# Three units of three experts in a new sequence, large GpSimd operations on VectorE, first unit mapped in order of use

## The chip, the core and the metric

The kernel runs on one core of one Trainium2 chip. The metric is device time in microseconds of one execution, from the median of several runs; less is better. The engines are named as in the profile: PE (TensorE), DVE (VectorE), ACT (ScalarE), POOL (GpSimd), SP (SyncE, which here issues most transfers).

## The reference

One layer of a diffusion backbone for 128 context tokens and 256 latent tokens (T = 384, D = 1024), in float32. A modulated input goes through a projection, four mLSTM heads and four Fourier groups, an output projection, and a LayerNorm; the second half is a routed mixture of 32 experts, four for each token, and a second LayerNorm.

```python
mix = jnp.concatenate([h_m, f_m], axis=-1) @ w_out
x = layer_norm(DEEPNORM_ALPHA * x + gate1 * mix, ln1_w, ln1_b)
u2 = x * (1.0 + scale2) + shift2
...
logits = xt.astype(F32) @ router_w.astype(F32) + router_b.astype(F32)
top_val, top_idx = lax.top_k(logits, TOP_K)
gates = jax.nn.softmax(top_val, axis=-1)
...
h = xblk @ w_gu[e] + b_gu[e]
x_glu, x_lin = jnp.split(h, 2, axis=-1)
x_glu = jnp.minimum(x_glu, SWIGLU_LIMIT)
x_lin = jnp.clip(x_lin, -SWIGLU_LIMIT, SWIGLU_LIMIT)
act = x_glu * jax.nn.sigmoid(SWIGLU_ALPHA * x_glu) * (x_lin + 1.0)
return act @ w_down[e] + b_down[e]
...
x = layer_norm(DEEPNORM_ALPHA * x + gate2 * y, ln2_w, ln2_b)
```

The modulation (shift, scale, gate) comes from SiLU(cond) through a linear map, with one cond for context tokens and one for latent tokens. Each expert has w_gu of 1024 x 2048 (8 MB) and w_down of 1024 x 1024 (4 MB).

## The kernel before

**Front, 0 to 244 us.** The projections run with the operands split into a high part and a low part (fp32r), three products for each. `halves_of` splits the input projection's weights (ACT L119, DVE L120); `wo_split(i, part)` does it for w_out: eight high halves as copies on ACT (L247), eight low halves as subtractions of 128x1024 on POOL (L249). `proj_N(3, ...)` computes the output gate's projection and calls three groups of work between its matmuls: Fourier stages (`fourier_A`, `fourier_B`), the heads' norms, `mod_rest` and `wo_split`. `mod_rest` (L668 to L674) makes the second half's modulation rows in a small tile `sm` on DVE and writes them to memory (`dab`) from ACT's queue, to be read back as rows broadcast over all partitions. `heads_T` transposes the gated heads (PE L597). The output projection (L853) is worked off as rows of eight steps for three token blocks (0 is the context) and two column halves; `out_half` adds the residual (DVE L860, L862, L864), `out_norm` normalises (ACT), and for block 0 the map with context scale and shift follows in two halves on POOL (L886, L887). `turn` transposes for the router, `router` multiplies (L918), `top4` picks four experts (DVE L923 to L946), `places` counts (PE L950, L951), `places_0` and `gather_0` (L977, L985) gather the tokens of experts 0 and 1, the first unit, so that they can start before the sort is done. The order of the steps from there on is written out as a string of step names (L1016).

**Places and units.** The experts 2 to 31 are sorted by their number of tokens and fill 30 places of fixed capacity; experts 0 and 1 have the first two. Capacities are grouped to units of 128 slots:

```python
KINDS = dict(A=[128], B=[96, 32], C=[64, 64], D=[64, 32, 32], E=[32] * 4)
SEQUENCE = "DACBACBACBACACCE"
```

The first unit, [64, 64], stands ahead of the sequence: 17 units, 32 places. A place ranks by its capacity, so the sequence sets when an expert of which size runs. Its weights are fetched through registers loaded with its number.

**Expert loop, L1327 to L1410.** For place i: SP queues the gate/up weights of place i + 2 (`load_gu`, four pieces of 2 MB) and the down weights of place i + 1 (`load_dn`, two pieces of 2 MB), all of them issued at L755 into a ring of eight slots of 2 MB; an issue waits until PE has finished with the piece that was in its slot. PE computes `gate_up` of place i (L1163, its bias L1171 or L1167), `spread` of finished units back to the tokens (L1241, added by DVE L1246; for the first unit with the experts' down bias, L1239), and `down` of place i - 1 (L1222). A unit's tokens are gathered two units at a time (`gather_two`, L1107). The first unit's gathered tokens are mapped with scale and shift (`modulate`, ACT L796 for the first four blocks of 128 rows, DVE L794 for the other four, and an addition of the context part, L797); expert 0 multiplies them in the order 2, 3, 0, 1, 4 to 7.

For expert 0 the second half of the down weights lies outside the ring, in two tiles of other pools (`w0` and `y1`, L781 and L782); the first half takes ring slots.

**Final rows.** At place 28 (i == NE - 4) a ring slot is taken for `fb`, four rows broadcast over the partitions for the last norm. A transfer of one element per partition into it (L1353) marks it as written, and at the end of the place `final_row` fills it (PE L1309 into PSUM, ACT L1310 into fb):

```python
if i == NE - 4:
    fb = slot(4, 1024, hold=True)[0]
    SP.dma_start(fb[:, 0, 0:1], bcast(ln2_w[:, 0:1]))
```

`fold` (L1317 to L1321, on DVE and POOL) folds the residual into the sum, `last_down` and `spread_last` (L1414, L1394) end the last place.

## Time and profile before

| | |
|---|---|
| median of 3 runs | 1246.8 us (1244.35, 1246.8, 1248.54) |
| profiled execution, own time | 1248.78 us |
| its span | 1247.1 us |
| PE busy | 1167.6 us (94%) |
| DVE, ACT, POOL busy | 446.4, 229.0, 69.3 us |
| read from HBM | 448.91 MB |
| mean transfer rate over the span | 363 GB/s |
| expert 0's first matmul | 244.17 us |

The times in the rows below are microseconds from the start of the span. A row of a timeline has the start, the duration, engine, line of the kernel, operation, what is written and read by the program's names, and in brackets how long the engine stood idle before and on whom it waited. The share of busy time is a mean over stages with different limits: the stages are told apart by the answers by stretches, which give each engine's busy time, the granted clock of PE (1.00 is 2.4 GHz, 0.50 is 1.2 GHz) and what the transfers moved. The waits of SP's queue tell why a transfer is not issued earlier.

### The profile page before, as it was taken

Reading aid. Unit: us, or ns where it says so; the run is one execution under the profiler, and the core shown is the slowest. Engines: PE = TensorE matmul, PEld = TensorE weight load, DVE = VectorE, ACT = ScalarE, POOL = GpSimd, SP = SyncE. Lnnn points to the kernel's source line nnn. Section 1 sums busy time; section 2 is a strip of 40 time slices with the busy share of each in tenths; the row PEclk is TensorE's granted clock in tenths of the full one; section 3 lists DMA queues with packets and bytes.
Section 4 is the critical chain, followed back from the end, with each engine's and each line's share of the span. In section 5 each row is a group of like instructions: output and inputs, shape, how many; then the busy total and the mean of one; then the engine's idle time right before and its main releaser. Section 6 shows DMA issues by size and latency. Waiting matters only on the chain.

```text
span 1247.1 us, 16409 instructions
## 1 busy us (share of the span) xinstructions
PE 1167.6 (94%) x6628; PEld 556.8 (45%) x6628; DVE 446.4 (36%) x944; ACT 229.0 (18%) x418; POOL 69.3 (6%) x79
## 2 busy tenths in 40 slices
PE   7999989799999999999999999999999999993874
PEld 4876768535335433434343353334435345331321
DVE  4444684623112431414323142332234124130415
ACT  2333341311211110201111121011111111111112
POOL 2001042200000000000000000000000000000301
PEclk9999989899899999999999999999999999996988
DMA  9977546499999999999999999999999899999993
GB/s 324 391 277 263 216 174 255 156 389 406 404 416 417 416 417 417 416 407 414 415 362 409 414 363 358 419 416 362 363 417 398 301 391 403 406 418 403 401 410 118
DMA packets 96978, 452.71 MB, mean 363 GB/s; under 512 B 8308, under 2 KB 18760, under 8 KB 62084
## 3 DMA queue, kind: packets, MB, share of 16 engines
q1 hardware_dynamic: 95088, 450.04, 91.0%
q10 hardware_dynamic: 1268, 1.31, 0.3%
q8 instruction: 54, 0.88, 0.3%
q0 software_dynamic: 544, 0.29, 0.1%
q14 instruction: 24, 0.20, 0.0%
HBM read 448.91 MB, written 2.70 MB: 362 GB/s over the span
## 4 chain that ended last, share of the span: by engine, by line
PE 84%; DMA 7%; DVE 5%; ACT 2%; issue 1%; SPq 1%; ACTq 0%; DVEq 0%
PE b L1163 38%; PE b L1222 19%; PE b L1241 4%; PE p L422 3%; DMA w<-in_w_gate_up_dram 3%; PE b L1107 3%; PE b L1171 2%; PE pm L853 2%; DMA w<-in_ln_w_dram 2%; PE b L1196 2%; DMA w<-in_w_ada_dram 1%; PE k L353 1%; ACT y L1228 1%; PE a L220 1%; DVE y L1230 1%
## 5 line engine op out<-in xcount | busy, mean ns | idle before, releaser
L1163 PE MATMUL b<-w,XT 128*64 128x512 f32 (+1 forms) x2560 | 496.2, 604 | 30.5 <-ACT w L1310 19.7
L1163 PEld LDWEIGHTS b<-w,XT 128*64 128x64 f32 (+1 forms) x2560 | 143.6, 129 | 332.2 <-issue 294.4
L1222 PE MATMUL b<-w,aT 128*64 128x512 f32 (+1 forms) x1596 | 248.3, 515 | 3.3 <-DMA w<-in_w_down_dram 3.2
L1182 DVE TENSOR_SCALAR g<-b 128x512 f32<-128x512 f32 (+1 forms) x40 | 24.5, 612 | 373.7 <-PE b L1171 293.9
L1222 PEld LDWEIGHTS b<-w,aT 128*64 128x64 f32 (+1 forms) x1596 | 81.6, 128 | 156.7 <-issue 141.9
L1230 DVE SCALAR_TENSOR_TENSOR y<-b,gc,y 64x512 fp32r<-64x512 f32 (+1 forms) x88 | 57.4, 652 | 217.6 <-ACT y L1228 217.3
L1228 ACT ACTIVATE y<-b,gc 64x512 fp32r<-64x512 f32 (+2 forms) x100 | 58.7, 587 | 292.1 <-PE b L1222 254.6
L1183 ACT ACTIVATE b<-g 128x512 f32<-128x512 f32 (+1 forms) x40 | 21.5, 538 | 353.6 <-DVE g L1182 353.4
L1246 DVE TENSOR_TENSOR yacc<-yacc,b 128x512 f32<-128x512 f32 x90 | 55.0, 680 | 0.0
L1107 PE MATMUL b<-O,tH 128*128 128x256 f32 x192 | 47.7, 289 | 4.5 <-DVE y L1230 4.5
L1241 PE MATMUL b<-y,OT 128*128 128x512 f32 x192 | 49.9, 405 | 0.0
L1317 POOL TENSOR_TENSOR XT<-tL,tH 128x384 f32<-128x384 f32 x2 | 2.0, 1006 | 841.5 <-PE b L1163 841.5
L1107 PE MATMUL b<-O,tL 128*128 128x256 f32 x192 | 46.5, 283 | 0.0
L1241 PEld LDWEIGHTS b<-y,OT 128*128 128x128 f32 x192 | 35.7, 193 | 13.9 <-issue 5.9
L1107 PEld LDWEIGHTS b<-O,tH 128*128 128x128 f32 x192 | 36.7, 191 | 10.2 <-DVE y L1230 5.3
L120 DVE TENSOR_TENSOR lw<-w,hw 128x1024 fp32r<-128x1024 f32 x20 | 24.4, 1222 | 34.9 <-ACT hw L119 34.7
L1107 PEld LDWEIGHTS b<-O,tL 128*128 128x128 f32 x192 | 36.7, 191 | 0.0
L1171 PEld LDWEIGHTS b<-bgu,pick 128*128 128x128 f32 x224 | 28.0, 189 | 18.7 <-issue 18.7
L1197 ACT ACTIVATE aT<-b 128x512 f32<-128x512 f32 (+1 forms) x40 | 21.3, 534 | 76.2 <-PE b L1196 70.9
L853 PE MATMUL pm<-w,mH 128*128 128x512 f32 x96 | 33.0, 426 | 0.0
L1171 PE MATMUL b<-bgu,pick 128*128 128x256 f32 x224 | 32.8, 292 | 0.0
L422 PE MATMUL p<-hw,uH 128*128 128x512 f32 x72 | 29.7, 412 | 1.7 <-ACT kq L412 1.7
(380 smaller groups left out, 1086.5 us busy)
## 6 DMA issues: line engine op xcount, KB each, us to landing
w<-in_w_gate_up_dram SPq DMA_DIRECT2D x113, 2048.0 KB, 13.4
w<-in_w_down_dram SPq DMA_DIRECT2D x52, 2048.0 KB, 15.5
w<-in_w_gate_up_dram SPq DMA_DIRECT2D x30, 1024.0 KB, 13.5
w<-in_w_down_dram SPq DMA_DIRECT2D x22, 1024.0 KB, 16.6
w<-in_w_ada_dram SPq DMA_DIRECT2D x8, 2048.0 KB, 7.6
w<-in_w_ada_dram SPq DMA_DIRECT2D x8, 1024.0 KB, 8.9
w<-in_w_in_dram SPq DMA_DIRECT2D x4, 2048.0 KB
w<-in_w_out_dram SPq DMA_DIRECT2D x2, 2048.0 KB, 8.8
```

The costliest lines, as they stand in the source:

```text
L422: PE.matmul(p[b], x, y, start=(k == 0 and t == 0), stop=(k == 7 and t == 2))
L853: PE.matmul(pm, x, y, start=(n == 0 and t == (part == 0) and part != 1), stop=(n == 7 and t == 2 and part != 0))
L1107: PE.matmul((pl if b else pc)[:, jj], t[b][:, (2 * i + jj) * 128:(2 * i + jj + 1) * 128], O[:, b], start=(b < 2 and q == 0), stop=(b != 1 ...
L1163: PE.matmul(p[g_][m * h:m * h + m], XT[:, k, o:o + m], rhs, start=(n_ == 0), stop=False, skip_group_check=True)
L1171: PE.matmul(p[g_][:, 256 * h:256 * h + 256], pick[2][:, h], bgu[:, q, 256 * g_:256 * g_ + 256], start=False, stop=(q == 1), skip_group_che ...
L1182: DVE.tensor_scalar(g, pg_, LIMIT, None, op0=OP.min)
L1196: PE.transpose(p[:, cc], s["act"][i][:, cc * 128:(cc + 1) * 128], ident)
L1222: PE.matmul(q[m * h:m * h + m, :f], aT[:, k, o:o + m], w[:, h * f:(h + 1) * f], start=(k == 0), stop=(k == 7))
L1228: ACT.activation(hi if plain else hi.bitcast(FR), dst, AF.Copy, scale=g)
L1230: DVE.scalar_tensor_tensor(y[1][o:o + m, h * f:(h + 1) * f].bitcast(FR), dst, g, hi, op0=OP.mult, op1=OP.subtract)
L1241: PE.matmul(p, OT[:, b * 128:(b + 1) * 128], y[q][:, hf * 512:(hf + 1) * 512].bitcast(FR), start=(u != 0 and q == 0), stop=(q == 1))
L1246: DVE.tensor_add(a, a, p)
```

## The change

The sequence of units is written anew: the unit of four experts (E) is gone, and there are three units of three (D), second, ninth and last; the multiset of capacities (five of 128, three of 96, fifteen of 64, nine of 32) is as before. The low halves of w_out are subtracted on DVE instead of POOL, six of them somewhat later; `mod_rest` stands ahead of two Fourier stages; the context map is two steps X and Y on DVE; O1 and g10 stand ahead of P2; expert 0's down weights are queued in the other order; the first unit is mapped ahead of the bias table's split, blocks 2 and 3 first; the one-element transfer into fb is a memset on POOL.

```diff
@@ -35,8 +35,8 @@
 
 
 
-KINDS = dict(A=[128], B=[96, 32], C=[64, 64], D=[64, 32, 32], E=[32] * 4)
-SEQUENCE = "DACBACBACBACACCE"
+KINDS = dict(A=[128], B=[96, 32], C=[64, 64], D=[64, 32, 32])
+SEQUENCE = "DACBACADBACCACBD"
 PARTS = {32: [(0, 4)], 64: [(0, 2)], 96: [(0, 2), (64, 4)], 128: [(0, 2), (64, 2)]}
 
 
@@ -246,7 +246,7 @@
         if part == 0:
             ACT.activation(h, w, AF.Copy)
         else:
-            POOL.tensor_sub(l, w, h.bitcast(FT))
+            DVE.tensor_sub(l, w, h.bitcast(FT))
 
     todo = [f for name in "qvzo" for f in halves_of(win[name])]
     cut = []
@@ -692,10 +692,9 @@
         head_out(2)
         for i in range(2):
             wo_split(i, 0)
-            wo_split(i, 1)
-        proj_N(3, ev_o, lambda: (mod_loads(), fourier_B(0), fourier_A(2), head_norm(1), head_out(3), wo_split(2, 0), wo_split(2, 1), wo_split(3, 0), wo_split(3, 1)),
-               lambda: (fourier_B(1), fourier_A(3), mod_rest()),
-               lambda: (fourier_B(2), head_norm(2), head_norm(3), fourier_B(3)))
+        proj_N(3, ev_o, lambda: (mod_loads(), fourier_B(0), fourier_A(2), head_norm(1), head_out(3), wo_split(2, 0), wo_split(3, 0)),
+               lambda: (mod_rest(), fourier_B(1), fourier_A(3), wo_split(2, 1), wo_split(3, 1)),
+               lambda: (fourier_B(2), head_norm(2), head_norm(3), fourier_B(3), wo_split(0, 1)))
         ACT.dma_start(new_n[0, 0].rearrange("d h p -> h d p"), nn.rearrange("h (d p) -> h d p", d=2))
         bc = {}
 
@@ -709,6 +708,7 @@
         for gr in range(4):
             split(fo[gr], mH[:, 4 + gr], mL[:, 4 + gr])
         heads_T()
+        wo_split(1, 1)
         wo[1].append(ring(8, 512).bitcast(FR))
         for i in range(4, 8):
             wo_split(i, 0)
@@ -773,7 +773,7 @@
                 src = w_dn[0, ex, :, i * 512:(i + 1) * 512].rearrange("o (k p) n -> p (o k) n", p=128)
                 WT["d", j, i] = fill(slot(8, 512), src, parts)
             return
-        for i in range(2):
+        for i in (1, 0) if j == ORDER[0] else (0, 1):
             src = w_dn[0, ex, i * 512:(i + 1) * 512].rearrange("o (k p) n -> p (o k) n", p=128)
             if i and j == ORDER[0]:
 
@@ -882,9 +882,14 @@
             nc_ = p2.tile([128, D], FT, name="g1c")
             ACT.activation(nc_, tX[b], AF.Identity, bias=nm, scale=rs_)
             ACT.dma_start(dx, nc_)
-            for hs in halves:
-                POOL.tensor_mul(tX[b][:, hs], nc_[:, hs], bc["A", 1][:, hs])
-                POOL.tensor_add(tX[b][:, hs], tX[b][:, hs], bc["D", 1][:, hs])
+            context.append(nc_)
+
+        context = []
+
+        def context_map(hf):
+            hs = halves[hf]
+            DVE.tensor_mul(tX[0][:, hs], context[0][:, hs], bc["A", 1][:, hs])
+            DVE.tensor_add(tX[0][:, hs], tX[0][:, hs], bc["D", 1][:, hs])
 
 
         def fold_1():
@@ -1011,9 +1016,9 @@
 
         m2_, h2, t1, t2 = out_rows(2, 1, {}, 1), out_half(2, 1), top4(1), top4(2)
         steps = dict(m=lambda: (next(m2_, 0), next(m2_, 0)), h=lambda: next(h2, 0), a=lambda: next(t1, 0), b=lambda: next(t2, 0),
-                     A=lambda: weave(t1), B=lambda: weave(t2), S=sort_1, C=lambda: DVE.tensor_copy(cnts, pp[:32, 3]), E=experts)
+                     A=lambda: weave(t1), B=lambda: weave(t2), S=sort_1, X=lambda: context_map(0), Y=lambda: context_map(1), C=lambda: DVE.tensor_copy(cnts, pp[:32, 3]), E=experts)
         next(m2_)
-        for step in "P0 m m T1 m O0 R1 m g00 N1 h h T2 g01 a h a h a N2 a a a a R2 P1 b b b b b b b O1 P2 g11 A g10 O2 B C S g20 g21 E".split():
+        for step in "P0 m m T1 m O0 X R1 m g00 Y N1 h h T2 g01 a h a h a N2 a a a a R2 P1 b b b O1 b b b b g10 P2 A g11 O2 B C S g20 g21 E".split():
             if step in steps:
                 steps[step]()
             else:
@@ -1030,6 +1035,16 @@
         itm = late2.tile([32, 2, ITEMS], FT, name="itm")
         iti = late2.tile([1, ITEMS + 1], I32, name="iti")
         mo = ctx.enter_context(tc.tile_pool(name="mo", bufs=2, reuse_waits="tile"))
+        XT0 = mo.tile([128, 2, 8, 128], FT, name="XT", bufs=1)[:, 0]
+
+        for i, j in ((0, 2), (0, 3), (1, 4), (1, 5), (2, 2), (0, 0), (0, 1), (1, 6), (1, 7), (2, 0), (2, 4), (2, 6)):
+            p, a = xt[j // 4][:, j % 4], [aff[:, q, j:j + 1] for q in range(2)]
+            if i == 0:
+                ACT.activation(XT0[:, j], p, AF.Identity, bias=a[0], scale=a[1])
+            elif i == 1:
+                DVE.tensor_scalar(XT0[:, j], p, a[1], a[0], op0=OP.mult, op1=OP.add)
+            else:
+                DVE.tensor_add(XT0[:, j:j + 2], XT0[:, j:j + 2], xc[j // 4][:, j % 4:j % 4 + 2])
 
         bgu = mo.tile([128, 2, 512], FR, name="bgu", bufs=1)
         raw = mo.tile([128, 512], FT, name="aT", bufs=1)
@@ -1043,9 +1058,6 @@
         POOL.dma_start(rows[0:4], dab[3].rearrange("c (h n) -> (c h) n", h=2))
         POOL.dma_start(rows[4:6], ln2_w.rearrange("o (h n) -> (o h) n", h=2))
         POOL.dma_start(rows[6:8], ln2_b.rearrange("o (h n) -> (o h) n", h=2))
-        XT0 = mo.tile([128, 2, 8, 128], FT, name="XT", bufs=1)[:, 0]
-        for i in range(2):
-            modulate(XT0[:, 4 * i:4 * i + 4], 4 * i, xt[i], xc[i], i)
         sort_1b()
 
 
@@ -1350,7 +1362,7 @@
         if i and i + 2 < NE:
             if i == NE - 4:
                 fb = slot(4, 1024, hold=True)[0]
-                SP.dma_start(fb[:, 0, 0:1], bcast(ln2_w[:, 0:1]))
+                POOL.memset(fb[:, 0, 0:1], 0.0)
             list(load_gu(ORDER[i + 2]))
         if i and i + 1 < NE:
             load_dn(ORDER[i + 1])
```

On DVE, around `mod_rest` in the projection of the output gate, before (`sm` are the modulation rows, `W` the folded Fourier tables, `og` the gated heads, `p_...` the gate's projection in PSUM):

```order
L671 COPY sm<-sm 64x32
L672 COPY sm<-sm 32x32
L673 TENSOR_TENSOR sm<-sm 32x32
L625 TENSOR_TENSOR W_1362<-a,y_1356 128x129
L626 TENSOR_TENSOR W_1362<-a,y_1356 128x127
L625 TENSOR_TENSOR W_1362<-a,y_1356 128x65
L626 TENSOR_TENSOR W_1362<-a,y_1356 128x63
L591 TENSOR_SCALAR og<-nm,mv 128x128 x6
L625 TENSOR_TENSOR W_1383<-n,y_1377 128x129
L626 TENSOR_TENSOR W_1383<-n,y_1377 128x127
L625 TENSOR_TENSOR W_1383<-n,y_1377 128x65
L626 TENSOR_TENSOR W_1383<-n,y_1377 128x63
```

The same stretch after, from the third operation on `sm` on, with the low halves of w_out (`w<-w`, L249) in it:

```order
L671 COPY sm<-sm 64x32
L672 COPY sm<-sm 32x32
L673 TENSOR_TENSOR sm<-sm 32x32
L625 TENSOR_TENSOR W_1323<-a,y_1317 128x129
L626 TENSOR_TENSOR W_1323<-a,y_1317 128x127
L625 TENSOR_TENSOR W_1323<-a,y_1317 128x65
L626 TENSOR_TENSOR W_1323<-a,y_1317 128x63
L249 TENSOR_TENSOR w<-w 128x1024 x2
L625 TENSOR_TENSOR W_1360<-a,y_1354 128x129
L626 TENSOR_TENSOR W_1360<-a,y_1354 128x127
L625 TENSOR_TENSOR W_1360<-a,y_1354 128x65
L626 TENSOR_TENSOR W_1360<-a,y_1354 128x63
```

The operations on `sm` stand ahead of the Fourier pieces L625 and L626 that they stood behind, and two subtractions follow the first of these; a third stands ahead of L492, five more behind L600.

On ACT, the queue that holds the transfer of the modulation rows (`dab<-sm`), before, with two of the Fourier copies (L621) and the table load of the gate's activation:

```order
L621 ACTIVATE y_1314<-a 128x194
L612 ACTIVATE E<-n 128x388
L674 DMA dab<-sm 64x5x32
L621 ACTIVATE y_1356<-a 128x194
L128 ACTIVATE mv<-mv,cst 128x3
L129 ACTIVATE mv<-mv 128x3
L128 ACTIVATE mv<-mv,cst 128x3
L129 ACTIVATE mv<-mv 128x3
L621 ACTIVATE y_1377<-n 128x194
L491 ACT_TABLE_LOAD
```

And after:

```order
L674 DMA dab<-sm 64x5x32
L621 ACTIVATE y_1317<-a 128x194
L612 ACTIVATE E<-n 128x388
L621 ACTIVATE y_1354<-a 128x194
L128 ACTIVATE mv<-mv,cst 128x3
L129 ACTIVATE mv<-mv 128x3
L128 ACTIVATE mv<-mv,cst 128x3
L129 ACTIVATE mv<-mv 128x3
L621 ACTIVATE y_1375<-n 128x194
L491 ACT_TABLE_LOAD
```

The transfer stands ahead of one more L621 and of L612, where it stood behind them; the rest is in the order of before.

On DVE, behind the sort of block 0 (`O_1490<-cst,code` are the places of a block's tokens in the first unit, `tX_69` is the context block), before:

```order
L867 BN_AGGR m_1475<-s_1476 128x2
L976 SCALAR_TENSOR_TENSOR code<-pp,sel 128x32
L977 TENSOR_TENSOR O_1490<-cst,code 128x128
L860 TENSOR_TENSOR pm<-pm,g_1502 128x512
L862 SCALAR_TENSOR_TENSOR tX_71<-tX_71,pm 128x512
L923 SCALAR_TENSOR_TENSOR tiny<-csb,m_1475,lg 128x32
```

And after:

```order
L867 BN_AGGR m_1475<-s_1476 128x2
L981 SCALAR_TENSOR_TENSOR code<-pp,sel 128x32
L982 TENSOR_TENSOR O_1490<-cst,code 128x128
L891 TENSOR_TENSOR tX_69<-g1c,prep 128x512
L892 TENSOR_TENSOR tX_69<-tX_69,Dc 128x512
L891 TENSOR_TENSOR tX_69<-g1c,prep 128x512
L892 TENSOR_TENSOR tX_69<-tX_69,Dc 128x512
L860 TENSOR_TENSOR pm<-pm,g_1502 128x512
L862 SCALAR_TENSOR_TENSOR tX_71<-tX_71,pm 128x512
```

The four operations of the context map, which stood on POOL (L886 and L887), stand here between the places of block 0 and L860 of block 2.

## Rows read from the trace of the kernel before

**Rows 1.** The page, part 1: busy time of each engine.

```profile
PE 1167.6 (94%) x6628; PEld 556.8 (45%) x6628; DVE 446.4 (36%) x944; ACT 229.0 (18%) x418; POOL 69.3 (6%) x79
```

**Rows 2.** Answer by stretches: window, length, busy per engine, PEclk, DMA share, GB/s.

```profile
275.00:625.00 350.00, 347.77 (x1961) 140.82 (x1958) 102.80 (x209) 49.59 (x90) 0.00 (x0) 0.98 1.01 413
330.00:348.00 18.00, 18.00 (x32) 5.42 (x32) 0.00 (x0) 2.99 (x5) 0.00 (x0) 0.53 1.01 418
625.00:1075.00 450.00, 447.77 (x2532) 186.35 (x2530) 140.68 (x279) 62.71 (x112) 0.00 (x0) 1.00 0.96 384
1150.00:1175.00 25.00, 24.03 (x212) 9.09 (x204) 5.85 (x12) 5.87 (x14) 11.27 (x12) 0.94 0.95 379
1175.00:1211.00 36.00, 25.45 (x152) 8.30 (x152) 14.14 (x22) 4.70 (x10) 1.63 (x2) 0.91 1.02 416
1222.00:1247.00 25.00, 8.03 (x32) 2.79 (x28) 15.59 (x27) 4.39 (x10) 5.88 (x4) 0.76 0.17 66
```

**Rows 3.** Waits of SP's queue, 625 to 1075 us: total, times, longest.

```profile
SPq L755 <- PE b L1163: 244.2, 61, 15.4
SPq L755 <- PE b L1222: 132.8, 31, 9.7
```

**Rows 4.** Timeline of PE: first matmuls of places 10 and 20, both 128.

```profile
531.03 3.65 PE L1163 MATMUL b<-w,XT 128*64 128x512 f32 x16
...
855.00 3.65 PE L1163 MATMUL b<-w,XT 128*64 128x512 f32 x16
```

**Rows 5.** Waits of ACT, 1100 to 1200 us.

```profile
ACT w L1310 <- DMA w<-in_ln_w_dram: 22.4, 1, 22.4
```

**Rows 6.** Timeline of PE: first matmul of place 29.

```profile
1149.35 4.66 PE L1163 MATMUL b<-w,XT 128*32 128x512 f32 x24 [19.71 <-ACT w L1310]
```

**Rows 7.** Timeline of all engines, 160 to 179 us.

```profile
161.91 1.19 DVE L120 TENSOR_TENSOR lw<-w,hw 128x1024 fp32r<-128x1024 f32 x1
...
163.18 9.51 POOL L249 TENSOR_TENSOR w<-w 128x1024 fp32r<-128x1024 f32 x4 [36.41 <-DVE lw L120]
...
170.30 2.43 DVE L671 COPY sm<-sm 64x32 f32<-64x32 f32 x1
...
172.76 0.17 DVE L672 COPY sm<-sm 32x32 f32<-32x32 f32 x1
...
173.95 0.33 ACT L621 ACTIVATE y<-a 128x194 f32<-128x194 f32 x1 [10.93 <-DVE sm L673]
...
176.81 1.56 ACT L491 ACTIVATE p<-p 128x512 f32<-128x512 f32 x3
...
178.17 0.48 PE L597 MATMUL n<-cst,og 128*128 128x128 f32 x1 [5.75 <-DVE og L492]
```

**Rows 8.** Chain of waits, 140 to 262 us: start, duration, step.

```profile
205.88 2.10 PE pm L853 x9
...
222.34 3.05 PE pm L853 x8
```

**Rows 9.** Timeline of all engines, 214 to 246 us.

```profile
217.11 1.03 DVE L932 SCALAR_TENSOR_TENSOR sel<-tiny,cst 128x32 f32<-128x32 f32 x1
...
221.24 0.56 PE L950 MATMUL pp<-sel,cst 128*128 128x32 f32 x2 [2.89 <-DVE sel L940]
...
228.64 0.70 DVE L860 TENSOR_TENSOR pm<-pm,g 128x512 f32<-128x512 f32 x1 [3.99 <-PE pm L853]
...
233.58 0.24 DVE L932 SCALAR_TENSOR_TENSOR sel<-tiny,cst 128x32 f32<-128x32 f32 x1
...
234.92 0.58 PE L950 MATMUL pp<-sel,cst 128*128 128x32 f32 x2 [1.72 <-DVE code L976]
...
244.17 2.67 PE L1163 MATMUL b<-w,XT 128*64 128x512 f32 x8 [3.14 <-issue]
```

**Rows 10.** Timeline of PE: down matmuls (L1222) of places 1 and 2, 64 slots each.

```profile
311.38 7.09 PE L1222 MATMUL b<-w,aT 128*64 128x512 f32 x32
...
342.51 9.62 PE L1222 MATMUL b<-w,aT 128*64 128x512 f32 x32
```

## The prediction

> **What bounds the kernel now.** I read the page's busy table first [rows 1]: PE is busy 94% of the span, which would call it the bound everywhere; but that is an average, and the stages have to be taken apart. The answer by stretches does that [rows 2]. From 275 us to 625 us the transfers run at 413 GB/s, from 625 to 1075 at 384, at 1175 to 1211 at 416. PE is busy through all of it (447.77 of 450 us in the second stretch). At 416 GB/s an expert's six pieces of 2 MB (four of gate/up, two of down: 12.58 million bytes) take 30.2 us. The weights are all in at about 1222 us; the 25 us behind that move 66 GB/s and are the tail. So the end is set by when the last weight lands, and that moves only by what the transfers lose: 450 x (1 - 384/416) = 34.6 us in the middle, 25 x (1 - 379/416) = 2.2 us at 1150 to 1175, 2.5 us from 275 to 625, and with whatever shifts the start of the expert loop at 244 us.
>
> Why do transfers pause while the queue has more to fetch? The waits of SP's queue say it [rows 3]: in 625 to 1075 its weight issues wait 61 times for a gate/up matmul (L1163) and 31 times for a down matmul (L1222), that is for a ring slot that PE has not released. In that stretch PE is behind the stream. Elsewhere it is ahead.
>
> So the order of the units matters: PE spends about the same on each unit of 128 slots, the stream spends 30.2 us on each expert, and a unit holds one to four experts. Two starts of a unit A [rows 4] lie six units apart (A C B A C B): (855.00 - 531.03) / 6 = 54.0 us of PE for a unit. A (one expert) puts PE 54.0 - 30.2 = 23.8 us further behind the stream, B and C (two) 6.4 us further ahead, D (three) 36.6 us ahead, E (four) 66.8 us ahead. What the stream loses is the highest point that this balance reaches.
>
> **The change part by part. Sequence.** Balance after u units holding n experts: 54.0u - 30.2n, the first unit (two experts) included. Before, D A C B A C B A C B A C A: the highest point is after 14 units and 24 experts, 756.0 - 724.8 = 31.2 us. That this is the right account is seen in the 34.6 us that the middle stretch loses [rows 2]. After, D A C B A C A D B A C C A: the highest point is after eight units and 14 experts, 432.0 - 422.8 = 9.2 us; D and B bring it to -34, and the last A ends, after 14 units and 25 experts, at 756.0 - 755.0 = 1.0. Gain: 31.2 - 9.2 = **22.0 us**. The measured loss exceeds the balance by 3 to 6 us (34.6, or 37.1 with the first stretch, against 31.2); if the new peak has the same excess the gain stays 22, if the excess vanishes it is 28. Downwards: behind the new peak the balance falls by 43 us, and the ring's eight slots of 2 MB hold 40 us of stream, so PE will wait for weights some 3 us in the new D and B; it stands at 4 instead of 1 after the last A, still under 9.2, and costs nothing. I take 22, bounds 11 (the new peak is twice as high, PE's unit costing 55.4 us in those eight) and 28.
>
> **The placeholder of the final rows.** At place 28 PE stands still for 19.71 us behind ACT L1310, which waits 22.4 us for a one-element transfer of ln2_w (L1353) that is queued behind weights [rows 5, 6]. A memset on the idle POOL takes its place; it waits for nothing but the old user of that slot, which was consumed long before. The standstill goes, but PE is ahead of the stream there, so only the slots it released late count: the 2.2 us of [rows 2] at 1150 to 1175. I take **2.2**, bounds 0 (PE then waits for the same weights) and 5.
>
> **The front, first part (163 to 184 us).** While POOL does four low halves of w_out (9.51 us, 2.4 us each), a copy of 64x32 on DVE takes 2.43 us, and 0.17 us once POOL is done [rows 7]. The small operations of mod_rest take 9 us in this way; ACT's queue holds a transfer from mod_rest's result ahead of its L621, which waits 10.93 us, and behind that come the table load and the gate's activation; PE idles 5.75 us before L597. The change takes the low halves from POOL and puts the transfer ahead of two L621 in ACT's queue. What is late next is the end of the projection itself at 172.4: from ACT's L491 to PE's L597 it is 178.17 - 176.81 = 1.36 us, so PE resumes near 173.9, 4.3 us earlier. What is added to DVE: eight subtractions of 1.19 us [rows 7]. Two lie before the gate in DVE's idle time behind the shortened mod_rest, one between W and L492, and five (6 us) ahead of the first L860; the rows that wait for that one, the turns at 196 us, are 7 us away, so they cost nothing while that margin lasts, up to 1.4 if it doesn't. Behind such gaps PE runs at the lower clock (1.2 GHz) for a while: in the one at 221 us eight L853 take 3.05 us, where nine took 2.10 [rows 8], so 1.2 us are lost each time. With a gap of 1.5 us that may go or stay. I take **5.5**, bounds 0 and 7 (the whole gap and the clock).
>
> **The front, second part (214 to 244 us).** The context map on POOL lies beside top4 of block 0: L932 takes 1.03 us there and 0.24 without POOL, with L934 and L936 some 2.9 us in all; PE's L950 waits 2.89 us for it [rows 9]. As steps X and Y on DVE the map comes behind the sort of block 0, where DVE waited 3.99 us for PE (four operations of 128x512 like the 0.70 us of L860, 2.8 us: they fit): gain 2.9. The half clock behind that gap gives 1.2 [rows 8]. The gather g10 (1.05 us) fills 1.72 us in which PE waits for block 2's positions, less 0.4 for O1 now in the middle of that chain: 0.6. Expert 0 starts 3.14 us after PE's last sort step, because ACT splits the bias table first and then maps k = 0 to 3 in one go, while expert 0 begins with k = 2, 3; now those are mapped first, two operations and one addition of a pair after the last gather: I estimate 1.8 of the 3.14 [rows 9]. Together **6.5**, bounds 3 and 8. What this moves back is the bias split; its first reader is the bias matmul at 262 us, 20 us on. Down weights of expert 0: the halves that need no ring slot go out first; the other four megabytes wait for PE's slots anyway, nothing either way. Of the front PE's time is the path (slots of the ring are released by PE's L853 and L1163), so its 12.0 us pass to the end one for one.
>
> Sum: 22.0 + 2.2 + 5.5 + 6.5 = 36.2 us off the profiled run's 1248.78 gives 1212.6. That run lay 2.0 over the median of 1246.8; against the median the forecast is **1211**.
>
> The Trainium skill has a rule that speaks against this. "SBUF — State Buffer", section "A bandwidth-pool intuition that's wrong", gives HBM to one core about 358 GB/s; by it an expert takes 35.1 us, no unit order would leave PE behind, and the sequence would give nothing (1233). The stretches at 413 to 418 GB/s [rows 2] decide against it.
>
> **Rivals.** (a) *The front gives little* (3 us): something else ends the two gaps, say the transfers of the modulation rows or the added DVE work. For it: three engines hand over within 2 us there. 1211 + 9 = 1220. (b) *The sequence gives half*: the new peak is near 20 us, since four of the eight units ahead of it are the first ones, with the sort and the first spread beside them, and the 54.0 us of a later unit don't show these. 1222. (c) *Half clock in the new D units.* In the first D, PE ran at 0.53 of full clock from 330 to 348 us, the down of 32 matmuls in 9.62 us instead of 7.09 [rows 2, 10]: about 9 us in 18. In the middle D that makes 1 + 3 + 9 = 13 after the last A, 4 above the peak; in the last D it lies before the tail, up to 9. 1215 to 1224, say 1219. Against it: the stretch in the first D follows the spread of the first unit with its 32-row bias matmuls (L1239), which the other D units lack; the E at the end, waiting for weights, had 0.94 and 0.91 [rows 2]. The Trainium skill ("TensorE: Matmul & The Clock Gate", section "HAM oscillation — how this bites in real kernels") says that short bursts of matmuls between waits for transfers start each at the low clock; by it this case is the one. The 0.94 at 1150 to 1175 [rows 2] disagrees. (d) *Slower.* PE at half clock through the whole middle D and B: 108 us there become longer by a factor between 1.36 (9.62/7.09) and, if all of it slows by the clock, 1/0.53 = 1.89, by 39 to 96 us. After the last A the balance is then 43 to 100, and the stream loses 34 to 91 us more: 1245 to 1302, about 1265 in between. It decides for slower once PE loses over 41 us there. Against it: after 19.71 us of standstill the clock is back soon after PE's restart at 1149.35 [rows 6] (a mean of 0.94 over 25 us is some 3 us at half clock). (e) *The sequence does nothing*, the stream being limited by something else that SP's waits hide: 1233; the waits in [rows 3] leave little room.
>
> **How the numbers follow.** Forecast (1200 to 1219) 0.60; (a) 0.12; (b) 0.12; (c) 0.12; (d) 0.03; (e) 0.01. The forecast's lower edge has the sequence's 28 and the front's upper bounds (1211 - 6 - 4 = 1201), its upper edge the lower half of the front. Range: 1199 to 1227 leaves out (d), (e) and the edges. A measurement of this kernel tells about 0.3% (3.7 us) from no change; all cases but (d) are faster by far more: faster 0.96, same 0.01, slower 0.03.
>
> **What would show it.** Sequence: transfers at about 408 GB/s or more over the stretch 625 to 1075 (a loss near 10 us, all of it before some 660 us), SP's longest waits for L1163 around the second A of "A C A", and PE waiting for weights a few us in the middle D. Placeholder: no wait of ACT in final_row, PE busy through place 29. Front: expert 0's first matmul near 232 us instead of 244.17, DVE's mod_rest under 2 us, the gap before L597 under 2 us. It is wrong if expert 0 starts after 240 (rival a), if the middle stretch still loses over 20 us (b), or if long half-clock stretches follow the middle D (c, d).

## The result, and the profile after

The changed kernel takes 1214.8 us (median of four runs, 1211.5 to 1217.3) against 1246 for the kernel before; the ratio is 0.9747 with a 95% interval of 0.9713 to 0.9781, so 31.5 us less (27 to 36). The forecast was 1211, 36 us less; the measured time lies in its range. The sum came out 4.7 us too large, and the runs below show where most of that lies: the two large terms were met within 2 us, and the hole in the transfers near the end, which the small third one (2.2 us) was to close, got larger instead.

Line numbers from about L700 on shift by some dozen: L1163 is L1175 now, L1222 is L1234, L950 is L955, L1309 is L1321. The page's first part, and the answer by stretches (columns as in [rows 2]), the stretches of before shifted by 10 us or more:

```profile
PE 1166.3 (96%) x6628; PEld 553.6 (46%) x6628; DVE 457.2 (38%) x966; ACT 229.3 (19%) x418; POOL 50.9 (4%) x68
```

```profile
265.00:615.00 350.00, 347.77 (x1975) 143.47 (x1972) 105.34 (x213) 51.74 (x93) 0.00 (x0) 0.98 1.02 413
615.00:1065.00 450.00, 443.14 (x2519) 183.23 (x2521) 139.53 (x285) 60.60 (x108) 0.00 (x0) 1.00 1.00 406
...
1114.00:1123.00 9.00, 9.00 (x32) 2.36 (x28) 0.00 (x0) 0.46 (x2) 0.24 (x1) 0.74 0.56 205
```

PE's busy time is what it was (1166.3 against 1167.6 us, [rows 1]); the share rose because the span shrank. The middle stretch runs at 406 GB/s instead of 384: it loses 450 x (1 - 406/416) = 10.8 us, where it lost 34.6. The third line is new: for nine us around 1118 the transfers run at 205 GB/s, 9 x (1 - 205/416) = 4.6 us lost, twice what the hole at 1150 to 1175 had cost before (2.2 us). Between 1065 and 1100 us they run at 404 GB/s, which loses 1.0 us more.

In the front (timeline of DVE and PE; the last two are the ends of the two parts that the prediction priced):

```profile
160.79 0.17 DVE L671 COPY sm<-sm 64x32 f32<-64x32 f32 x1
...
170.16 0.33 PE L597 MATMUL n<-cst,og 128*128 128x128 f32 x1 [0.64 <-DVE og L492]
...
207.29 0.24 DVE L937 SCALAR_TENSOR_TENSOR sel<-tiny,cst 128x32 f32<-128x32 f32 x1
...
208.99 0.30 PE L955 MATMUL pp<-sel,cst 128*128 128x32 f32 x2
...
228.97 3.65 PE L1175 MATMUL b<-w,XT 128*64 128x512 f32 x16 [1.23 <-DVE XT L1047]
```

The copy of 64x32 takes 0.17 us (2.43 in [rows 7]), PE waits 0.64 us for the gated heads instead of 5.75, not at all for the positions of block 0 (2.89 in [rows 9]), and expert 0 starts at 228.97 instead of 244.17. Of these 15.2 us, 2.9 lie ahead of everything that the change touches (the gate's projection ended at 172.42, now at 169.52) and are chance: other profiles of kernels whose front is that of before had this end at 169.4 to 169.6 too. From that end to expert 0 it was 71.7 us and is 59.4: 12.3 us less. One profile gives this to some 3 us: with the front of before it is 71.7 in s1_sequence and 68.9 in s2_memset, with the changed front 59.4 in s3_front and 57.9 in s4_transfer and s6_later.

### The profile page after: what moved, and what is told of

It is laid out like the page before. It is cut to its first block, busy times and chain, and to the rows that moved or that the text cites. A ratio compares the mean times of both kernels' runs of the same rounds, so it can differ in the third digit from the quotient of the medians.

```text
span 1215.1 us, 16415 instructions
## 1 busy us (share of the span) xinstructions
PE 1166.3 (96%) x6628; PEld 553.6 (46%) x6628; DVE 457.2 (38%) x966; ACT 229.3 (19%) x418; POOL 50.9 (4%) x68
## 4 chain that ended last, share of the span: by engine, by line
PE 72%; DMA 6%; DVE 5%; ACT 1%; issue 1%; POOL 0%; SPq 0%; DVEq 0%; ACTq 0%; POOLq 0%
PE b L1175 37%; PE b L1234 19%; DMA w<-in_w_gate_up_dram 5%; PE b L1253 3%; PE b L1119 3%; PE b L1183 2%; DMA w<-in_w_down_dram 2%; PE b L1208 2%; PE pm L853 1%; ACT y L1240 1%; DVE y L1242 1%; PE b L1251 1%; PE b L1144 1%; PE b L1321 1%; PE b L1142 1%
## 5 line engine op out<-in xcount | busy, mean ns | idle before, releaser
L1175 PE MATMUL b<-w,XT 128*64 128x512 f32 (+1 forms) x2560 | 497.2, 603 | 9.7 <-DMA w<-in_w_gate_up_dram 8.5
L1175 PEld LDWEIGHTS b<-w,XT 128*64 128x64 f32 (+1 forms) x2560 | 143.4, 129 | 313.3 <-issue 289.7
L1234 PE MATMUL b<-w,aT 128*64 128x512 f32 (+1 forms) x1596 | 247.1, 512 | 1.0 <-DMA w<-in_w_down_dram 0.8
L1234 PEld LDWEIGHTS b<-w,aT 128*64 128x64 f32 (+1 forms) x1596 | 80.7, 127 | 153.9 <-issue 138.6
L1240 ACT ACTIVATE y<-b,gc 64x512 fp32r<-64x512 f32 (+3 forms) x100 | 58.7, 587 | 290.5 <-PE b L1234 250.6
L1150 DVE COPY gc<-b 64x1 f32<-64x1 f32 (+1 forms) x104 | 16.2, 156 | 46.5 <-ACT OT L1145 45.2
L853 PE MATMUL pm<-w,mH 128*128 128x512 f32 x96 | 31.5, 407 | 0.3 <-DVE tX L862 0.2
```

What stands on the lines that cost most here:

```text
L853: PE.matmul(pm, x, y, start=(n == 0 and t == (part == 0) and part != 1), stop=(n == 7 and t == 2 and part != 0))
L1175: PE.matmul(p[g_][m * h:m * h + m], XT[:, k, o:o + m], rhs, start=(n_ == 0), stop=False, skip_group_check=True)
L1234: PE.matmul(q[m * h:m * h + m, :f], aT[:, k, o:o + m], w[:, h * f:(h + 1) * f], start=(k == 0), stop=(k == 7))
L1240: ACT.activation(hi if plain else hi.bitcast(FR), dst, AF.Copy, scale=g)
```

## The experiments

**What each part gives alone.** Three kernels carry one part each, a fourth lacks one.

The sequence alone:

```diff
-SEQUENCE = "DACBACBACBACACCE"
+SEQUENCE = "DACBACADBACCACBD"
```

> The kernel before with the new sequence alone; the front and the one-element transfer into fb stay. Theory of the prediction (terms add up): the sequence gives 22 us, so 1246 - 22 = 1224, the stretch 625 to 1075 loses about 11 us instead of 34.6, the hole in the transfers at place 29 stays about 2 us. Rival (the terms don't add up): after the new order PE is nearer to the stream at place 28 than before, the balance there being 864 - 875.8 = -11.8 against a peak of 9.2, so that the 20 us of standstill at the final rows, some 8 us of their matmuls and 3 us of half clock bring PE behind the stream a second time: a hole of 12 to 16 us at place 29 and about 1236 to 1240.

Measured: 1228.5 us, ratio 0.9862 (0.9845 to 0.9878), 17 us less. The answer by stretches and the waits of ACT on the final rows (L1310):

```profile
615.00:1065.00 450.00, 441.80 (x2515) 186.68 (x2515) 143.98 (x292) 62.92 (x112) 0.00 (x0) 1.00 1.00 406
1065.00:1110.00 45.00, 45.00 (x282) 13.87 (x274) 11.40 (x21) 3.72 (x7) 1.02 (x1) 1.00 1.00 402
1110.00:1135.00 25.00, 23.52 (x101) 7.19 (x99) 3.72 (x7) 7.63 (x15) 1.00 (x1) 0.80 0.82 316
```

```profile
ACT w L1310 <- PE b L1309: 2.9, 1, 2.9
```

The middle gains what was forecast; the whole run gains 17 us where 22 were forecast. A hole of 25 x (1 - 316/416) = 6.0 us opens at place 29, where 2.2 were lost before. Neither theory had it in that size for that reason: the wait for the one-element transfer, 22.4 us in [rows 5], is not in the list any more. The rival fell in its main mechanism (no standstill), yet it named the place that costs, and with the final rows' matmuls and the half clock two things that the runs below find there.

The memset alone:

```diff
-                SP.dma_start(fb[:, 0, 0:1], bcast(ln2_w[:, 0:1]))
+                POOL.memset(fb[:, 0, 0:1], 0.0)
```

> The kernel before with the memset into fb in place of the one-element transfer, nothing else. Theory of the prediction: the standstill of 19.7 us goes, and the hole of 2.2 us in the transfers at 1150 to 1156 with it: 1246 - 2 = 1244. Rival: the hole is made by the held ring slot and the final rows' own matmuls, not by the standstill, and PE merely waits for the same weights: 1246.

Measured: 1242.9, ratio 0.9977 (0.9964 to 0.9989), 2.9 us less (1.4 to 4.5); the hole is gone:

```profile
1105.00:1145.00 40.00, 35.32 (x230) 13.25 (x229) 11.34 (x34) 7.25 (x14) 6.67 (x8) 0.91 1.02 417
1145.00:1175.00 30.00, 18.06 (x140) 5.27 (x132) 8.74 (x13) 3.33 (x8) 7.27 (x8) 0.78 1.02 417
```

So on the old sequence this part is worth what the forecast gave it. The changed kernel with the transfer put back:

```diff
-                POOL.memset(fb[:, 0, 0:1], 0.0)
+                SP.dma_start(fb[:, 0, 0:1], bcast(ln2_w[:, 0:1]))
```

> The changed kernel with the one-element transfer back in place of the memset. Theory of the prediction (terms add up): 2 us slower than the changed kernel, 1217. Rival (terms don't add up): PE's 20 us of standstill now fall where PE is only some 20 us ahead of the stream, and the transfers lose 10 to 15 us more at place 29: 1225 to 1230.

Measured: 1216.9, ratio 0.9769 (0.9752 to 0.9786), which overlaps the changed kernel's 0.9713 to 0.9781: no difference that can be told. ACT's wait and the issue on SP's queue there, and for comparison the issue in the kernel before (start, duration of the issue):

```profile
ACT w L1322 <- DMA w<-in_ln_w_dram: 2.5, 1, 2.5
```

```profile
1094.92 0.35 SPq L1365 DMA_DIRECT2D w<-in_ln_w_dram  x1
```

```profile
1113.88 10.53 SPq L755 DMA_DIRECT2D w<-in_w_down_dram  x3
1124.52 9.52 SPq L1353 DMA_DIRECT2D w<-in_ln_w_dram  x1
```

Before, SP came to the small transfer at 1124.52, as PE started the final rows (1124.01), because the weights ahead of it were still being issued. On the new sequence it goes out six us ahead of the final rows (1101.11), and ACT waits 2.5 us. So the two parts overlap: the sequence takes the standstill away by itself, and the memset has little left to give.

The front alone (all other edits, with the old sequence and the transfer):

> The changed front (subtractions and context map on DVE, the transfer of the modulation rows earlier, g10 and O1 earlier, first unit mapped in order of use, down halves of expert 0 in the other order) with the old sequence and the old one-element transfer. Theory: 12 us off, all of it kept to the end: 1234, expert 0's first matmul near 232. Rival: part of the front's gain is lost again in the ring at 275 us and the gain at the end is 6 or less: 1240.

Measured: 1233.8, ratio 0.9896 (0.9879 to 0.9913), 13 us less, expert 0 at 230.63. The three parts alone give 17 + 3 + 13 = 33 us, the whole 31.5: within the intervals the same.

**Which edit of the front.** The low halves on DVE, mod_rest left where it was:

```diff
-            POOL.tensor_sub(l, w, h.bitcast(FT))
+            DVE.tensor_sub(l, w, h.bitcast(FT))
...
-        proj_N(3, ev_o, lambda: (mod_loads(), fourier_B(0), fourier_A(2), head_norm(1), head_out(3), wo_split(2, 0), wo_split(2, 1), wo_split(3, 0), wo_split(3, 1)),
-               lambda: (fourier_B(1), fourier_A(3), mod_rest()),
+        proj_N(3, ev_o, lambda: (mod_loads(), fourier_B(0), fourier_A(2), head_norm(1), head_out(3), wo_split(2, 0), wo_split(3, 0)),
+               lambda: (fourier_B(1), fourier_A(3), mod_rest(), wo_split(2, 1), wo_split(3, 1)),
...
```

> The kernel before with the low halves of w_out on DVE at the places of the changed kernel; mod_rest stays behind the Fourier stages, all else as before. Theory (POOL beside DVE makes the small operations of mod_rest slow): they take about 1.2 us instead of 9.3, PE's gap before L597 falls from 5.75 to 1 or 2 us, 5 us less at the end: 1241. Rival (the place of the transfer in ACT's queue makes the gap): the gap stays above 4 us, 1246.

Measured: 1240.6, ratio 0.9964 (0.9943 to 0.9985), 4.5 us less. And the order alone, the low halves still on POOL:

```diff
-               lambda: (fourier_B(1), fourier_A(3), mod_rest()),
+               lambda: (mod_rest(), fourier_B(1), fourier_A(3)),
```

> The kernel before with mod_rest ahead of two Fourier stages, as in the changed kernel, and the low halves still on POOL. Theory (POOL beside DVE is the cause): mod_rest still takes about 9 us, PE's gap before L597 stays 4 to 6 us: 1245. Rival (the transfer's place in ACT's queue): the gap falls under 2 us, 1241.

Measured: 1249.9, ratio 1.0032 (1.0016 to 1.0047), 4 us slower. Timeline rows of the first, then of the second:

```profile
163.32 0.17 DVE L671 COPY sm<-sm 64x32 f32<-64x32 f32 x1
...
171.56 0.33 PE L597 MATMUL n<-cst,og 128*128 128x128 f32 x1 [0.17 <-DVE og L492]
```

```profile
160.81 9.32 POOL L249 TENSOR_TENSOR w<-w 128x1024 fp32r<-128x1024 f32 x4 [36.42 <-DVE lw L120]
...
165.51 2.36 DVE L671 COPY sm<-sm 64x32 f32<-64x32 f32 x1
...
172.40 0.99 PE L618 MATMUL a<-E,dft 128*128 128x194 f32 x2 [8.09 <-DVE W L626]
```

The subtraction's engine decides: with POOL idle the copy takes 0.17 us and PE waits 0.17 instead of 5.75. With POOL busy the order makes it worse: the ten us of mod_rest now stand ahead of the Fourier pieces on DVE, and PE waits 8.09 us for these in the middle of the projection. Neither forecast came. The gap before L597 did fall under 2 us (0.52 at most), as the rival said, but only because PE had waited already; the time rose by 4 us, where the rival had 5 less and the theory no change.

The context map alone (steps X and Y on DVE):

> The kernel before with the context map as steps X and Y on DVE alone; string of steps else as before, POOL idle there. Theory: L932, L934 and L936 of block 0 take 0.24 to 0.28 us each, PE's wait before L950 of block 0 (2.89 us) goes, and the half clock behind it: 4 us from the projection of the gate to expert 0, about 1242. Rival: the four operations on DVE take back what they give: 1246.

Measured: 1240.9, ratio 0.9960 (0.9945 to 0.9975), 5 us less.

```profile
212.31 0.24 DVE L937 SCALAR_TENSOR_TENSOR sel<-tiny,cst 128x32 f32<-128x32 f32 x1
...
214.01 0.30 PE L955 MATMUL pp<-sel,cst 128*128 128x32 f32 x2
```

The wait of 2.89 us is gone and nothing is taken back.

**The hole at place 29.** In the changed kernel PE's timeline there reads:

```profile
1104.41 5.19 PE L1321 MATMUL b<-cT,cst 8*128 8x512 f32 x14
1110.60 2.07 PE L1321 MATMUL b<-cT,cst 4*128 4x512 f32 x2 [0.99 <-DVE y L1242]
1112.60 3.68 PE L1175 MATMUL b<-w,XT 128*64 128x512 f32 x8
```

Between the down of place 27 and place 29 stand 8.2 us of final rows, matmuls over 8 or 4 partitions, and behind them eight matmuls of place 29 take 3.68 us, twice the 1.9 of other places. The final rows moved one place on:

```diff
-        if i == NE - 4:
+        if i == NE - 3:
             for at, r in enumerate((0, 1, 4, 5)):
                 final_row(at, r, fb)
```

> The changed kernel with the four final rows of place 28 computed at the end of place 29 instead; the ring slot is still held from place 28. Theory: the hole at 1114 to 1123 is a second peak of PE's balance, made by the 8.2 us of final rows and the half clock behind them, ahead of place 29's first release: it goes down from 4.6 to 0 or 1 there, and comes back at most in part at place 30, where experts are short: about 1211. Rival: the held ring slot or the 96-token down ahead makes the hole: it stays at 4 to 5, 1215.

Measured: 1216.4, ratio 0.9770 (0.9719 to 0.9821), no difference to the changed kernel.

```profile
1100.00:1125.00 25.00, 25.00 (x183) 9.86 (x182) 8.02 (x22) 5.18 (x10) 0.00 (x0) 1.00 1.02 416
...
1160.00:1180.00 20.00, 17.12 (x56) 5.23 (x60) 8.53 (x11) 2.78 (x5) 4.24 (x3) 0.74 1.03 398
```

The hole at place 29 is gone (416 GB/s), though the ring slot is held as before: without the final rows the held slot makes no hole. Whether it takes part in the hole when the rows are there is open, since no run has the rows without the held slot. What was won there did not reach the end; the clock's mean is 0.74 in the last places. The same matmuls over 96 partitions, the added ones zero (two memsets on POOL make them):

```diff
...
-            PE.matmul(p, ident[lo:lo + n_, c_:c_ + 1].to_broadcast([n_, 128]), src, start=True, stop=True)
+            PE.matmul(p, ident[0:96, c_:c_ + 1].to_broadcast([96, 128]), cTr[:, 0:512], start=True, stop=True)
...
-                    PE.matmul(p, cT[:, 1, b], bdn[:, hf * 512:(hf + 1) * 512], start=True, stop=False)
+                    PE.matmul(p, cTr[:, T + 128 * b:T + 128 * b + 128], bdn[:, hf * 512:(hf + 1) * 512], start=True, stop=False)
...
```

> The changed kernel, with the matmuls of the final rows (8 or 4 partitions) and of the first unit's bias in spread (32 partitions) run over 96 partitions, the added ones being zero: same count of matmuls, same columns streamed. Theory: matmuls over few partitions bring the clock down although PE is busy, and the half-clock stretches at 315 to 335, 1108 to 1119 and 1177 to 1183 us are theirs. Then all three are gone, the final rows at place 28 and the first quarter of place 29's gate/up take some 4 us less, the hole in the transfers at 1114 to 1123 shrinks from 4.6 to about 1, the tail shortens by 2: about 1209. Rival: the clock falls for another reason (waits, small tiles): the stretches stay, 1215.

Measured: 1213.1, ratio 0.9749 (0.9708 to 0.9790), no difference. In the three stretches that the expectation names the half clock was gone, but the two memsets on POOL ahead of the bias table's transfers held up expert 0. First the issue of these transfers in the changed kernel; then, in this run, the memset, the issue, ACT's split of the table and PE in expert 0 (timelines):

```profile
215.72 2.24 POOL L1052 DMA_DIRECT2D aT<-in_b_gate_up_dram  x4 [46.11 <-DVE pm L860]
```

```profile
227.76 0.73 POOL L1035 MEMSET cT<- 32x768 f32 x1 [56.56 <-PE lg L968]
...
229.22 2.23 POOL L1054 DMA_DIRECT2D aT<-in_b_gate_up_dram  x4
...
235.94 0.63 ACT L119 ACTIVATE bgu<-aT 128x512 fp32r<-128x512 f32 x1 [7.68 <-DMA aT<-in_b_gate_up_dram]
...
238.65 0.23 PE L1287 MATMUL b<-cl,cst 32*32 32x1 f32 x2 [5.99 <-DVE sc L975]
```

The memset waits for PE's L968, so the transfers go out 13.5 us later than in the changed kernel, and ACT splits the table at 235.94 instead of 227.30. With the memsets behind those transfers:

> The changed kernel with the final rows' and the bias matmuls over 96 partitions as in s5_rows96, but with the two memsets behind the transfers of the bias table, so that expert 0 isn't held up (there PE waited 5.99 us). Theory (balance of starts measured from the trace): the start of place 29 lies 4.8 us behind the stream's earlier peak in the changed kernel; the lower clock is 2 to 3 us of it and some 2 us more in the tail: hole 2 us, time 1211. Rival (the time at half clock is hidden anyway): 1215.

Measured: 1210.9, ratio 0.9718 (0.9693 to 0.9743). Two stretches of the changed kernel, then of this one (the first holds the bias matmuls of `spread`, the second the final rows):

```profile
315.00:335.00 20.00, 20.00 (x40) 6.07 (x40) 0.10 (x1) 3.17 (x6) 0.00 (x0) 0.57 1.01 416
...
1105.00:1125.00 20.00, 19.00 (x65) 6.54 (x65) 3.75 (x9) 7.45 (x15) 1.00 (x1) 0.74 0.81 322
```

```profile
315.00:335.00 20.00, 20.00 (x116) 7.21 (x114) 1.73 (x3) 4.74 (x8) 0.00 (x0) 1.00 1.01 416
...
1105.00:1125.00 20.00, 20.00 (x79) 7.56 (x81) 5.29 (x17) 7.58 (x16) 1.01 (x1) 1.00 0.97 386
```

For the first stretch this does not show that the padding is the cause. In s1_sequence, s4_transfer and s6_later the bias matmuls run over 32 partitions, as in the changed kernel, and the clock stays at 1.00 there all the same; the other eight kernels with 32 partitions fall to half clock in that `spread`. The stretch in s4_transfer, and one of s8_rows96 a little later:

```profile
315.00:335.00 20.00, 20.00 (x104) 6.38 (x106) 1.73 (x3) 4.73 (x8) 0.00 (x0) 1.00 1.01 415
```

```profile
335.00:355.00 20.00, 14.81 (x96) 5.38 (x98) 3.62 (x8) 2.63 (x6) 0.00 (x0) 0.74 1.02 419
```

What s8_rows96 saves in `spread` it does not keep: PE then waits for weights in the first D (0.79, 3.07 and 1.32 us), the clock falls there instead, and at place 6 both kernels have the same distance to the stream (-17.4 and -17.7 us in the balance explained below). For the final rows the case is firmer. In the changed kernel, s1_sequence, s2_memset, s4_transfer, s6_later and s7_seq, where PE goes on behind them, the clock falls to half during them; over 96 partitions, in s5_rows96, s8_rows96 and s9_split, it does not.

The eight matmuls of place 29 behind the final rows, in s8_rows96 (timeline of PE):

```profile
1104.85 7.32 PE L1322 MATMUL b<-cT,cst 96*128 96x512 f32 x16
1112.10 1.94 PE L1177 MATMUL b<-w,XT 128*64 128x512 f32 x8
```

And with two of the four final rows at the end of place 29:

```diff
-        if i == NE - 4:
-            for at, r in enumerate((0, 1, 4, 5)):
+        if NE - 5 < i < NE - 2:
+            for at, r in ((0, 0), (1, 1)) if i == NE - 4 else ((2, 4), (3, 5)):
                 final_row(at, r, fb)
```

> s8_rows96, and of the four final rows two at the end of place 28 and two at the end of place 29. Theory: the two rows moved take 3.7 us from the peak at place 29, which so goes under the earlier one: no hole there, none at place 30, 1208 or 2 less than s8_rows96. Rival: the rows open a hole wherever they stand, as at the end of place 29 in s6_later: no change to s8_rows96.

Measured: 1209.1, ratio 0.9706 (0.9680 to 0.9731), the lowest median of all.

```profile
1105.00:1125.00 20.00, 20.00 (x112) 7.93 (x115) 5.75 (x18) 5.39 (x12) 0.00 (x0) 1.00 1.02 419
1125.00:1150.00 25.00, 25.00 (x178) 9.98 (x174) 13.46 (x22) 5.69 (x12) 6.60 (x5) 1.00 1.02 417
```

No hole at place 29 and none at place 30. The medians of these two lie 4 and 6 us under the changed kernel; their intervals still overlap with its own, so that they are faster than it is likely and not shown.

**A sequence with a lower peak on paper.**

```diff
-SEQUENCE = "DACBACADBACCACBD"
+SEQUENCE = "DACACDACABBCACBD"
```

> The changed kernel with the sequence D A C A C D A C A B B C A C B D: same units, balance 54.0u - 30.2n at most 1.0 after 14 units (places up to the last A) and -1.8 and -3.6 before, instead of 9.2. Theory (a late second peak at place 29 that is counted from the same balance): the middle loses 2 to 3 us instead of 10.8, and the hole at place 29 grows by what the middle no longer loses, from 4.6 to about 12: 1215, no gain. Rival (the hole at place 29 is a fixed loss of that place): 8 us less, 1207.

Measured: 1221.5, ratio 0.9816 (0.9774 to 0.9857), 7 us slower than the changed kernel where the theories had 0 and -8. The two intervals just touch, but each of its four runs (1220.3 to 1222.8) lies above all of the changed kernel's.

```profile
505.00:540.00 35.00, 35.00 (x166) 13.41 (x164) 9.55 (x15) 3.94 (x6) 0.00 (x0) 1.00 0.93 370
...
780.00:885.00 105.00, 102.42 (x683) 39.26 (x681) 38.48 (x88) 16.39 (x32) 0.00 (x0) 1.00 0.89 349
885.00:1100.00 215.00, 215.00 (x1222) 87.36 (x1220) 69.26 (x138) 29.32 (x52) 0.00 (x0) 1.00 1.02 417
```

At 780 to 885 the transfers lose 105 x (1 - 349/416) = 17 us, where the flat balance has nothing, and at 505 to 540 another 3.9. The balance read from the starts of PE (first matmul of a place, less that of place 0, less 30.2 us for each place) shows it:

| kernel | earlier peak | later peak | transfers lose between |
|---|---|---|---|
| before | -9.0 at place 2 | +29.9 at place 26 | 2.5 and 34.6 up to there |
| changed | +3.7 at place 27 | +7.8 at place 29 | 4.6 at place 29 |
| s8_rows96 | +5.1 at place 27 | +8.3 at place 29 | 1.4 at place 29 |
| s6_later | +4.6 at place 27 | +0.6 at place 29 | 0 at place 29 |
| s9_split | +5.3 at place 27 | +4.9 at place 29 | 0 at place 29 |
| s7_seq | -2.6 at place 10 | +12.6 at place 20 | 17 at 780 to 885 |

For place 29 of the changed kernel that is 1112.60 - 228.97 - 29 x 30.2 = +7.8. With the peaks paired as in the table, what the transfers lose follows their distance within 2 us. But the pairing is a choice, and the starts leave some us open: in the four kernels with the new sequence the start of place 15 stands at +6.4 to +7.2, above that of place 27, and against it the distance to place 29 is 0.7 us in the changed kernel, where 4.6 were lost. What holds the stream up is not the start of a place but the end of PE's work on a piece of weights. Counted so, from the last matmul on each piece of 2 MB against 5.03 us of stream for a piece (an estimate worked out from the trace), the changed kernel's balance is as high at place 13's last piece as at place 26's first (0.1 us apart) and 2.6 us higher at place 29's first. The slot that is held for fb from place 28 on takes up to 5.0 us more of the stream's cover; the 4.6 us measured lie between 2.6 and 7.6.

In s7_seq the unit B at places 18 and 19 lasts 77.3 us from its start to the next unit's (766.78 to 844.05): into it fall the down of the A ahead (13.95 us) and the gather of the next two units. The flat 54.0 us of a unit spreads these evenly; the peaks are made by where they fall.

## Why the forecast held, step by step

**The middle.** The account was a balance of PE against the stream, and its difference of two peaks (22.0 us) was met by the trace: the loss of the middle went from 34.6 to 10.8, 23.8 us. The single peaks were less exact than their difference, so that the close agreement is in part luck. Read from the starts, the balance at place 14 is +3.0 and not +9.2, and s7_seq shows that the flat unit cost cannot rank sequences that differ by some us: the two theories that were made with it for that sequence missed by 7 and 15 us.

**The end.** This is the term that was mis-sized. By the forecast's formula the balance is at 864 - 875.8 = -11.8 ahead of the last D; it took over from the old sequence that PE is ahead of the stream at place 28, added the 2.2 us of the placeholder as a gain, and saw no loss behind the middle. Measured is +7.8 at place 29, and a hole of 4.6 us where none was forecast; another 1.0 us is lost from 1065 to 1100. Against this the middle gave 1.8 us more than forecast. Of the difference of 20 us in the balance, 8.2 are the final rows with their wait, which were seen as hidden because PE is ahead there, and 5.2 are PE's waits for weights in the B behind the middle D (3.55 and 1.63 us of idle time in two stretches of 25 us from 740 to 790), where 3 were forecast; some 6 are left (12, if one counts from place 14, where the formula was 6.2 too high), perhaps the down and the gather that fall ahead of place 29, as in s7_seq, which no run separated. The half clock adds nearly 2 us behind the start (3.68 us for eight matmuls instead of 1.94). That there is no hole without the final rows is shown by s6_later. That the clock has a part in it is likely by s8_rows96, whose hole is 1.4 us: of the 3.2 us less, 1.7 are those eight matmuls, and 1.4 may be the earlier peak, which stands that much higher there. The standstill, which the term was about, was taken away by the sequence already (s1_sequence, s4_transfer); the prediction did not ask how SP's queue would stand at place 28 after the move.

**The front.** 12.0 us were forecast, 12.3 are in the trace from the projection's end to expert 0, and 13 (10.9 to 15.1) at the end in s3_front. By parts: up to PE's resumption 5.1 us, from there to the positions of block 0 from 43.07 to 38.83, 4.2 us, and on to expert 0 from 22.93 to 19.98, 2.9 us. The forecast had 4.3 for the first, 2.9 for the wait of block 0 with 1.2 for the clock behind the first gap, and 3.6 for the rest, so each part came within 0.8 us. It passed to the end one for one, as was argued, within the interval of s3_front. What was said of mod_rest's order was not needed for it: f1_subtract has the whole effect on the gap, and f2_order shows that the order alone costs 4 us.

One cover was thinner than said. The bias table's split was given 20 us of cover, to its reader at the bias matmul. But on DVE the steps of the sort stand behind it in the queue, and PE waits for these within expert 0: s5_rows96, where the table's split on ACT comes 8.6 us later (235.94 against 227.30), waits 5.99 us there. So the cover was under 3 us.

**The rivals.** (c), half clock in the new D units, did not come in a size that counts: the mean clock of 615 to 1065 is 1.00, and still 0.97 and 0.96 in the two stretches from 740 to 790 in which PE waits for weights. There it is at 0.50 from 763.7 to 767.1, behind waits for weights of 1.22 and 2.33 us. In the last D half clock came, with the final rows (0.74 at 1114 to 1123). The rule of the Trainium skill ("TensorE: Matmul & The Clock Gate", "HAM oscillation — how this bites in real kernels"), that bursts of matmuls between waits for transfers start at the low clock, has only a small case in the changed kernel, the stretch from 763.7 on, and a larger one in the first D of s8_rows96 (0.74 from 335 to 355, with three waits). The half clock of the first D, to which (c) pointed, is not explained: with the same matmuls it was there in the changed kernel and not in s1_sequence, s4_transfer and s6_later. (a), (b), (d) and (e) are excluded by the front's 12.3 us and the middle's 10.8.

## What to carry to other kernels

Where an engine and a stream take turns as the bound, write down the running balance of the two: only its highest point costs time, so lowering the first peak is worth at most the distance to the next one. Take that balance from the trace, best from the times at which the engine is done with each buffer, and not from a mean cost of a stage, since late parts of a stage fall behind its end; the starts of the stages read it to some us only. And when a small operation is many times slower than its like a few us later, look at which other engine was busy, before moving it in its queue.

## What the runs showed of the hardware

Final rows, matmuls over 8 or 4 partitions, brought half clock although PE had not rested: in six kernels the clock fell during them (0.74 of full clock at 1105 to 1125 us in the changed kernel). Over 96 partitions, with the same count of matmuls and the same columns, it stayed at 1.00 in three kernels, and the eight matmuls behind them take 1.94 instead of 3.68 us. What in the 96 partitions keeps the clock up was not looked into. For the bias matmuls over 32 partitions in `spread` the same is not shown: of eleven kernels with them the clock fell there in eight (0.57 at 315 to 335 us in the changed kernel) and stayed at 1.00 in three.

A subtraction of 128x1024 on POOL takes 2.38 us (9.51 for four), on DVE 1.2. Beside POOL's, DVE operations on `sm` take 2.05 to 2.43 us, a copy of 64x32 among them 2.36 to 2.43 instead of 0.17: about one POOL operation for each of these, whatever its size. Not every DVE operation is held so. The Fourier pieces, whose `a` lies in PSUM, started beside the same POOL operation in the kernel before and took their usual 0.2 to 0.3 us:

```profile
163.18 9.51 POOL L249 TENSOR_TENSOR w<-w 128x1024 fp32r<-128x1024 f32 x4 [36.41 <-DVE lw L120]
...
163.41 0.22 DVE L625 TENSOR_TENSOR W<-a,y 128x65 f32<-128x65 f32 x1
163.54 0.22 DVE L626 TENSOR_TENSOR W<-a,y 128x63 f32<-128x63 f32 x1
163.68 2.05 DVE L668 TENSOR_TENSOR sm<-sm 64x128 f32<-64x128 f32 x1
```
